# Decoder layer on one core: the residual seeds the down projection's banks, the last visits are reordered, and the weight tiles come from two pools

## The chip, the core and the metric

The kernel runs on 1 core of a Trainium2 chip. The metric is the device time of one execution in microseconds (us), as a median of runs. Five engines work side by side, each on its own list of instructions in program order: PE (TensorE, with its weight loads shown apart as PEld), DVE (VectorE), ACT (ScalarE), POOL (GpSimd) and SP (SyncE, which here issues most transfers). They wait for each other through semaphores. A transfer is issued by an engine's queue and carried by 16 DMA engines. SBUF is the memory that engines read, PSUM the banks in which TensorE accumulates.

## What is computed

One layer of a decoder, for a prompt of 512 tokens and for 8 samples of 4 tokens, with the same weights; T = 544 columns in all, in two halves of HT = 272. Attention, a gated delta rule and cross attention come first; the change lies in the feed-forward part and at the step into it:

```python
    x = x + xo @ p['w_xo']
    hf = rmsnorm(x, p['norm_ffn_g'])
    gate, up = jnp.split(hf @ p['w_gate_up'], 2, axis=-1)
    x = x + (jax.nn.silu(gate) * up) @ p['w_down']
```

The width of `x` is 2048 (KD = 16 row blocks of 128), the hidden width 5632 (NH = 44 blocks). The last `x +` is called the residual here. All of it is float32; a product of two float32 matrices is made as three products of their high and low parts, `wh*h + wh*l + wl*h`.

## The kernel before

**Into the feed-forward part.** `cross` ends with the projection `w_xo` in two parts (halves of the columns), each over m = 0 to 15: `weights` (L191) loads a tile `wr` on SP's queue (L195), ACT casts it to `wh` (L200), DVE makes `wl` (L201), TensorE multiplies (L1534), DVE adds the product to `x[m]` (L1537). Six of the sixteen weight pairs are kept from the first part to the second, in the pool `pb2`; the others come from the pool `w`. In the second part, as pairs of `x[m]` are ready, `Pair` makes the operands of the gate and up projection from them on DVE and ACT (L1586 to L1613). `x` itself is stored to `xT` in DRAM. When all of this is released, the pools `hp` and `wp` are opened over its space.

**Gate and up.** For each of the 44 hidden blocks a 2x2 block product is made in 7 products instead of 8, from sums of blocks. Each of the 7 is a tick of the plan: 24 matmuls of 128x128 by 128x272 (L1726; L1898 warms up). A weight tile goes raw (SP, L1702), `sum` (DVE, L1708), `wh` (ACT, L1715), `wl` (DVE, L1719). All of them are tiles of one size in the pool `wp`, in a ring of 13. The hidden rows go to `hT` in DRAM and come back as `pr` on POOL's queue (L1944).

**Down.** From tick 308 on, output rows are made in 8 blocks of two (m = 0, 2 ... 14), again by 7 products. A *step* is 42 matmuls (L1780) for one block and one of 11 groups of hidden rows: 88 steps. A step's weights: `raw` in two transfers (L1747), three sums on DVE (L1757 to L1759), two casts to `wh` on ACT (L1764), two `wl` on DVE (L1770). A *visit* is one or more steps of one block in a row. The products gather in four PSUM tiles, the banks P16, P7, P45 and P23. All blocks share the four, so each visit ends by taking them out to SBUF parts (`take`, L1820 adds on DVE, L1822 copies on ACT), and P45 and P23 are seeded with the next block's parts before its first product (`before`, L1802). At the last visit of a block `combine` (L1830 to L1837) joins banks and parts to the two output rows.

**Order.** `VISITS` lists (half, groups) and runs each entry over the half's four blocks. `LAST` is a last stage of end visits that alternate between block m with two steps and block m + 8 with one. There are 52 visits. Under a manual schedule, `at(tick, place, fn)` puts instructions in order by tick and then by place, on all engines alike; an engine never passes over one that waits.

**Residual.** In the two steps after the second visit of a block (the third for the other half), `residual` loads `xl` from `xT` (SP, L1846, two buffers of the tag `rstd`), POOL multiplies it by `r1` (L1851) and adds it to, or takes it off, the parts (L1853 to L1856).

**Output.** `store_y` (L2029): four transposes of a finished row to the one bank `aux` (L964), four scalings to `y` on ACT (L2036), a store (L2037); as a third piece two transposes of the sample columns (L2041), a scaling `ys` on DVE (L2043), a store (L2045). The row of P23 comes first, then that of P45.

## Time and profile before

| | before |
|---|---|
| median of 3 runs | 3003.34 us (3001.32 to 3003.95) |
| the profiled execution's own time | 3001.82 us |
| its span in the trace | 3000.1 us |
| mean granted TensorE clock | 0.988 |
| PE / PEld busy | 2881.7 us (96%) / 2772.6 us (92%) |
| DVE / ACT / POOL busy | 2096.9 us (70%) / 1490.5 us (50%) / 731.8 us (24%) |

The last matmul of `w_xo` starts at 1500.40 us of the span. Gate and up fill 1507 to 2460 us, down 2460 to 2988 us, and the last store ends the span at 3000.1 us.

How rows are read: a row of the stretches gives start and end, length, then for PE, PEld, DVE, ACT and POOL the busy us and the number of instructions, then the granted TensorE clock (1.00 is full), the busy share of the DMA engines and GB/s. (That share can read above 1.) A group row gives line, engine, operation, output <- inputs, shapes, count, busy us and mean ns of one. A row of waits gives who waited for whom, the us in total, how often and the longest.

### The profile page before, as it was taken

To read this page: it belongs to the slowest core of one execution; us is meant where nothing else is said; L and a number is where in the kernel's file an instruction comes from. 1 tells how busy PE (TensorE), PEld (TensorE's weight loads), DVE (VectorE), ACT (ScalarE), POOL (GpSimd) and SP (SyncE) were. 2 spreads that over 40 slices of the span, in tenths; PEclk is the share of its full clock that TensorE was granted. 3 is DMA by queue.
4 is the path that set the end of the run, shared out by engine and by line. 5 is a ranking of instruction groups with operands and counts; after the bars stand their busy time and mean duration, and the time that the engine had idled before them with its cause. 6 is when DMAs were issued, how large, how long until landed. Compare 5 with 4: busy or idle time off the path is not lost.

```text
span 3000.1 us, 56822 instructions
## 1 busy us (share of the span) xinstructions
PE 2881.7 (96%) x22122; PEld 2772.6 (92%) x22122; DVE 2096.9 (70%) x3302; ACT 1490.5 (50%) x2820; POOL 731.8 (24%) x932
## 2 busy tenths in 40 slices
PE   8999999999999999999979999999999999899997
PEld 7999998889899989998769999999999999899996
DVE  6776775655656664346588878888788877987765
ACT  5545443444555664345554444444444456455554
POOL 3211213312113100004213332333323333631100
PEclk9999999999999999999989999999999999999998
DMA  7323333454544674433444445454454459677542
GB/s 216 94 77 83 84 91 87 136 150 124 176 128 126 201 239 147 141 100 109 132 133 140 146 136 158 144 158 134 146 155 150 148 171 273 173 215 201 172 133 74
DMA packets 635814, 435.47 MB, mean 145 GB/s; under 512 B 35899, under 2 KB 566152, under 8 KB 635544
## 3 DMA queue, kind: packets, MB, share of 16 engines
q1 hardware_dynamic: 603720, 377.39, 43.0%
q0 software_dynamic: 22176, 42.90, 4.7%
q10 hardware_dynamic: 9648, 11.54, 1.1%
q8 instruction: 174, 2.85, 0.4%
q14 instruction: 96, 0.79, 0.1%
HBM read 355.61 MB, written 76.13 MB: 144 GB/s over the span
## 4 chain that ended last, share of the span: by engine, by line
PE 54%; DVE 5%; DMA 2%; issue 1%; ACT 1%; SPq 0%; DVEq 0%; ACTq 0%
PE gu L1726 30%; PE bank L1780 11%; PE mm L212 8%; DVE wl L1770 2%; PE aux L1346 2%; PE mm L1534 2%; DMA raw<-in_w_down 1%; PE aux L964 1%; DVE sum L1758 1%; PE aux L754 0%; DVE sum L1757 0%; DVE sum L1759 0%; DMA raw<-in_w_gate_up 0%; DVE a L1820 0%; PE aux L1420 0%
## 5 line engine op out<-in xcount | busy, mean ns | idle before, releaser
L1726 PE MATMUL gu<-pr,wh 128*128 128x272 f32 x4928 | 673.1, 289 | 13.1 <-ACT pr L1601 12.1
L1726 PEld LDWEIGHTS gu<-pr,wh 128*128 128x128 f32 x4928 | 639.6, 189 | 15.7 <-ACT pr L1601 13.3
L212 PE MATMUL mm<-ah,wh 128*128 128x272 f32 (+1 forms) x2464 | 537.8, 298 | 5.4 <-ACT ah L325 4.2
L212 PE MATMUL mm<-al,wh 128*128 128x272 f32 (+1 forms) x2464 | 523.3, 291 | 0.7 <-DVE al L243 0.6
L212 PE MATMUL mm<-ah,wl 128*128 128x272 f32 (+1 forms) x2464 | 515.0, 290 | 0.1
L1780 PE MATMUL bank<-pr,wh 128*128 128x272 f32 x2464 | 474.6, 291 | 12.6 <-ACT bank L1802 12.0
L212 PEld LDWEIGHTS mm<-ah,wh 128*128 128x128 f32 (+1 forms) x2464 | 391.1, 188 | 28.8 <-issue 8.5
L1780 PEld LDWEIGHTS bank<-pr,wh 128*128 128x128 f32 x2464 | 391.5, 191 | 14.6 <-ACT bank L1802 13.6
L201 DVE TENSOR_TENSOR wl<-wr,wh 128x512 fp32r<-128x512 f32 (+1 forms) x366 | 262.5, 721 | 194.7 <-ACT wh L200 185.4
L212 PEld LDWEIGHTS mm<-al,wh 128*128 128x128 f32 (+1 forms) x2464 | 388.7, 188 | 5.4 <-issue 2.0
L200 ACT CAST wh<-wr 128x512 fp32r<-128x512 f32 (+1 forms) x366 | 224.3, 615 | 333.2 <-PE mm L212 272.2
L212 PEld LDWEIGHTS mm<-ah,wl 128*128 128x128 f32 (+1 forms) x2464 | 385.4, 188 | 2.5 <-DVE wl L201 0.5
L1780 PE MATMUL bank<-pr,wl 128*128 128x272 f32 x1232 | 364.2, 296 | 18.7 <-DVE wl L1770 15.8
L1726 PE MATMUL gu<-pr,wl 128*128 128x272 f32 x2464 | 359.8, 288 | 1.3 <-DVE wl L1719 1.3
L1726 PEld LDWEIGHTS gu<-pr,wl 128*128 128x128 f32 x2464 | 328.9, 189 | 1.6 <-DVE wl L1719 1.6
L1719 DVE TENSOR_TENSOR wl<-sum,wh 128x1024 fp32r<-128x1024 f32 x176 | 215.9, 1226 | 83.5 <-ACT wh L1715 83.1
L1715 ACT CAST wh<-sum 128x1024 fp32r<-128x1024 f32 x176 | 185.0, 1051 | 164.2 <-DVE wl L1719 156.1
L1780 PEld LDWEIGHTS bank<-pr,wl 128*128 128x128 f32 x1232 | 235.2, 191 | 30.8 <-DVE wl L1770 30.6
L1719 DVE TENSOR_TENSOR wl<-raw,wh 128x1024 fp32r<-128x1024 f32 x132 | 201.3, 1525 | 5.2 <-ACT hs L1932 0.5
L1715 ACT CAST wh<-raw 128x1024 fp32r<-128x1024 f32 x132 | 138.9, 1053 | 95.7 <-DVE sum L1708 72.9
L1708 DVE TENSOR_TENSOR sum<-raw,sum 128x1024 f32<-128x1024 f32 x88 | 125.4, 1425 | 29.6 <-PE gu L1726 29.6
L1933 POOL TENSOR_TENSOR hs<-x,hs 128x544 fp32r<-128x544 f32 x44 | 86.3, 1962 | 184.2 <-ACT hs L1932 120.9
(524 smaller groups left out, 4397.4 us busy)
## 6 DMA issues: line engine op xcount, KB each, us to landing
raw<-in_w_gate_up SPq DMA_DIRECT2D x176, 512.0 KB
wr<-in_w_in SPq DMA_DIRECT2D x108, 512.0 KB
raw<-in_w_down SPq DMA_DIRECT2D x176, 256.0 KB
hT<-hs SPq DMA_DIRECT2D x154, 272.0 KB
pr<-hT POOLq DMA_DIRECT2D x154, 272.0 KB, 7.0
page<-in_cache_sb_k SPq DMA_DIRECT2D x128, 128.0 KB
page<-in_cache_sb_v SPq DMA_DIRECT2D x64, 256.0 KB
wr<-in_w_out SPq DMA_DIRECT2D x32, 512.0 KB
```

Of the source, the lines that this page charges most:

```text
L200: nc.scalar.copy(hi[:, :m, :n], raw[:, k : k + m, :n])
L201: nc.vector.tensor_sub(lo[:, :m, :n], raw[:, k : k + m, :n], hi[:, :m, :n].bitcast(F32))
L212: c.nc.tensor.matmul(ps[:n, h, :HT], l[:, :n], r[:, h * HT : (h + 1) * HT], start=first and i == 0, stop=last and i == 2,)
L1346: nc.tensor.matmul(ps[:, :256], l, r, start=k == 0 and n == 0, stop=k == 7 and n == 2)
L1534: nc.tensor.matmul(ps[:, 0, :HT], l, r[:, cols], start=k == 0 and i == 0, stop=k == 3 and i == 2)
L1708: self.f.c.nc.vector.tensor_sub(self.a[q], self.a[x], self.a[y])
L1715: self.f.c.nc.scalar.copy(self.hi[q], self.left(q))
L1719: self.f.c.nc.vector.tensor_sub(self.lo[q], self.left(q), self.hi[q].bitcast(F32))
L1726: self.f.c.nc.tensor.matmul(bank, w[:, i * P : (i + 1) * P], self.f.pairs[i].op[q][r], start=q in (1, 5) and n == 0, stop=n == 23, skip_gr ...
L1770: self.c.nc.vector.tensor_sub(lo, x, self.hi[i].bitcast(F32))
L1780: self.c.nc.tensor.matmul(self.c.bank[bank][:, o], t[x][:, s, i * P : (i + 1) * P], pairs[i].op[q][r], start=new and not (i or n), stop=se ...
L1933: at(tick, 80, lambda: c.nc.gpsimd.tensor_sub(lo[:, o : o + w], src[:, :w], hi[:, :w].bitcast(F32)))
```

## The change

1. The table of visits: the two-step entry of half 0 on groups 7 and 8 becomes two entries of one step, half 1 gets an entry of its own on group 8, and all end visits have two steps. 56 visits, 7 for each block.
2. `residual` is gone. `Ffn.start` runs eight times during gate and up: it loads two rows from `xT`, POOL multiplies both by `r1` and takes half of one off the other, and SP stores them to a DRAM tile `xq`. At a block's first visit, P45 and P23 are seeded from `xq` (`Down.load`, two buffers of the tag `rstd`); the order of products is then 4, 5, 1, 6, 7, 2, 3.
3. `take`: P16 and P7 always by DVE, as a copy the first time, P45 and P23 by ACT. `combine(0)` stands among the matmuls of the end visit's last step and not behind them, in two pieces; sums and the first `wl` of a step stand earlier in the tick.
4. Output: P45's row first, `ys` scaled on ACT, and the last block's transposes go to three banks that are free by then and not to `aux`.
5. Weight tiles: 9 in `wp` and 4 in a new pool `vp`, which holds every `wl` and the raw block "12". The pool `w` is opened earlier, so that other tiles of the phase before lie below the two; `weights` takes its `wh` and `wl` ahead of `wr`.

```diff
-VISITS = ((0, (0,)), (1, (0,)), (1, (1,)), (0, (1, 2)), (1, (2, 3)), (0, (3, 4)), (1, (4, 5)), (0, (5, 6)), (1, (6, 7)), (0, (7, 8)), (1, (8, 9)))
-LAST = (9, 10), (10,)
+VISITS = ((0, (0,)), (1, (0,)), (1, (1,)), (0, (1, 2)), (1, (2, 3)), (0, (3, 4)), (1, (4, 5)), (0, (5, 6)), (1, (6, 7)), (0, (7,)), (0, (8,)),
+          (1, (8,)))
+LAST = (9, 10), (9, 10)
...
 def weights(c, w, k0, nk, c0, n=P, kept=False, eng=None):
+    parts = [[(c.pb if kept else c.w).tile([P, 4, P], F32R, tag=x, name=x, bufs=XO_KEPT if kept else 4) for x in ("wh", "wl")] for _ in range(0, nk, 4)]
     raw = c.w.tile([P, 8, P], F32, tag="wr", name="wr", bufs=3)
...
-    self.a[x] = f.tile(F32, "raw")
+    self.a[x] = f.tile(F32, "raw", x == "12")
...
     def next_visit(self):
         self.visit += 1
-        self.order = (1, 6, 7, 4, 5, 2, 3) if self.visit == self.end else (4, 5, 2, 3, 1, 6, 7)
-        self.seeds = () if not self.visit else (P45, P23, P16, P7) if self.visit == self.end else (P45, P23)
+        self.order = (1, 6, 7, 4, 5, 2, 3) if self.visit == self.end else (4, 5, 2, 3, 1, 6, 7) if self.visit else (4, 5, 1, 6, 7, 2, 3)
+        self.seeds = (P45, P23, P16, P7) if self.visit == self.end else (P45, P23)
+    def load(self, bank):
+        self.x = self.x if bank == P23 else {}
+        self.x[bank] = self.c.cst.tile([P, T], F32, tag="rstd", name="xl", bufs=2)
+        self.c.nc.sync.dma_start(self.x[bank], self.f.xq[self.m + (bank == P45)])
     def before(self, bank):
         if bank in self.seeds:
-            self.c.nc.scalar.copy(self.c.bank[bank], self.parts[bank])
+            self.c.nc.scalar.copy(self.c.bank[bank], self.parts[bank] if self.visit else halves(self.x[bank]))
...
     def take(self, bank):
         new, x = bank not in self.parts, self.part(bank)
-        if bank in (P16, P7) and not new:
+        if bank in (P45, P23):
+            self.c.nc.scalar.copy(x, self.c.bank[bank])
+        elif new:
+            self.c.nc.vector.tensor_copy(x, self.c.bank[bank])
+        else:
             self.c.nc.vector.tensor_add(x, x, self.c.bank[bank])
-        else:
-            self.c.nc.scalar.copy(x, self.c.bank[bank])
...
+        for m in range(0, KD, 2):
+            for step, place in enumerate((3, 79, 2)):
+                at(38 + 14 * m + 3 * step, place, lambda m=m, step=step: self.start(m, step))
...
-        return self.c.wp.tile([P, 8 * P], dt, tag="w", name=name, bufs=W_TILES)
+        return (self.c.vp if own else self.c.wp).tile([P, 8 * P], dt, tag="w", name=name, bufs=4 if own else W_TILES - 4)
...
+    def start(self, m, step):
+        c, g = self.c, self.c.nc.gpsimd
+        if step == 0:
+            self.x = [c.tt("xr") for _ in range(2)]
+            for i, x in enumerate(self.x):
+                c.nc.sync.dma_start(x, c.xT[m + i])
+        elif step == 1:
+            for x in self.x:
+                g.tensor_mul(x, x, self.r1)
+            y, z = self.x
+            g.tensor_sub(y[:, HT:], y[:, HT:], z[:, HT:])
+        else:
+            for i, x in enumerate(self.x):
+                c.nc.sync.dma_start(self.xq[m + i], x)
...
-        at(early(2), 45, s.sums)
+        at(early(2), 25, s.sums)
         for i in range(2):
             at(early(1), 20 + i, lambda i=i: s.high(i))
-            at(early(1), 50 + i, lambda i=i: s.low(i))
+            at(early(1), (31, 50)[i], lambda i=i: s.low(i))
         if p == 0:
-            at(tick, 28, lambda: (self.c.open_banks(), b.next_visit()))
+            at(tick, 28, lambda: (self.c.open_banks(), b.next_visit(), seed(b, P45, P23)))
+            at(tick - 4, 62, lambda: b.load(P45))
+            at(tick - 1, 62, lambda: b.load(P23))
...
+        if nb and nb.m not in self.begun:
+            self.begun.add(nb.m)
+            for bank in (P45, P23):
+                at(*((tick - 1, 62) if p else (tick, 29)), lambda bank=bank: nb.load(bank))
...
         if s.visit == b.end:
-            at(tick, 47, lambda: (b.combine(0), seed(P16, P7)))
-            at(tick, 60, lambda: (b.combine(1), seed(P45)))
-            at(tick, 61, lambda: (b.combine(2), seed(P23), self.out(tick, b)))
+            at(tick, 32.2, lambda: b.combine(0))
+            at(tick, 33.2, lambda: b.combine(0.5))
+            at(tick, 34, lambda: seed(nb, P16, P7))
+            at(tick, 60, lambda: (b.combine(1), seed(nb, P45)))
+            at(tick, 61, lambda: (b.combine(2), seed(nb, P23), self.out(tick, b, nb is None)))
...
-        if s.visit == 1 + (b.m >= 8):
-            b.residual(tick)
...
-        done = [(b.m, b.flat[P23]), (b.m + 1, b.flat[P45])]
+        done = [(b.m + 1, b.flat[P45]), (b.m, b.flat[P23])]
...
+            self.work.at(t, x, lambda i=i: store_y(self.c, done, i, self.c.spare[i] if last else None))
...
+    ps = c.aux() if ps is None else ps
...
-    nc.vector.tensor_scalar(t[:NS, : 2 * P], ps[:NS, : 2 * P], c.unscale[:NS, 4:5], None, ALU.mult)
+    nc.scalar.activation(t[:NS, : 2 * P], ps[:NS, : 2 * P], AF.Identity, scale=c.unscale[:NS, 4:5])
...
     phase = ExitStack()
+    c.w = phase.enter_context(tc.tile_pool(name="w", bufs=3))
     c.pc = phase.enter_context(tc.tile_pool(name="pc", bufs=1))
...
-    c.hp, c.wp = (ctx.enter_context(tc.tile_pool(name=x, bufs=3)) for x in ("hp", "wp"))
+    c.hp, c.vp, c.wp = (ctx.enter_context(tc.tile_pool(name=x, bufs=3)) for x in ("hp", "vp", "wp"))
```

First place: SP's list where the feed-forward part begins, before the change. `wr` are the last weights of `w_xo`, `raw` the first of gate and up.

```order
L195 DMA wr<-in_w_xo 128x4x128
L1473 DMA xv<-in_cache_mem_v 128x512 x3
L195 DMA wr<-in_w_xo 128x4x128 x3
L1702 DMA raw<-in_w_gate_up 128x8x128 x15
L1935 DMA hT<-hs 128x544 x3
```

The same place of the changed kernel:

```order
L198 DMA wr<-in_w_xo 128x4x128
L1476 DMA xv<-in_cache_mem_v 128x512 x3
L1705 DMA raw<-in_w_gate_up 128x8x128 x3
L198 DMA wr<-in_w_xo 128x4x128 x3
L1705 DMA raw<-in_w_gate_up 128x8x128 x12
```

Three raw tiles of gate and up now stand ahead of the last three tiles of `w_xo`.

Second place: SP's list around the first steps of down, before the change. `raw` are the steps' weights (two rows to a step), `hT` the last hidden rows on their way out.

```order
L1935 DMA hT<-hs 128x544 x2
L1747 DMA raw<-in_w_down 128x4x128 x6
L1935 DMA hT<-hs 128x544
L1747 DMA raw<-in_w_down 128x4x128 x2
L1935 DMA hT<-hs 128x544 x2
L1747 DMA raw<-in_w_down 128x4x128 x4
L1935 DMA hT<-hs 128x544 x2
L1747 DMA raw<-in_w_down 128x4x128 x2
L1935 DMA hT<-hs 128x544 x2
L1747 DMA raw<-in_w_down 128x4x128 x16
L1846 DMA xl<-xT 128x544
L1747 DMA raw<-in_w_down 128x4x128 x2
```

The same place of the changed kernel; `xl` are the prepared residual rows:

```order
L1750 DMA raw<-in_w_down 128x4x128 x2
L1807 DMA xl<-xq 128x544 x6
L1750 DMA raw<-in_w_down 128x4x128 x2
L1807 DMA xl<-xq 128x544 x2
L1750 DMA raw<-in_w_down 128x4x128 x2
L1944 DMA hT<-hs 128x544
L1807 DMA xl<-xq 128x544 x2
L1750 DMA raw<-in_w_down 128x4x128 x2
L1944 DMA hT<-hs 128x544 x2
L1807 DMA xl<-xq 128x544 x2
L1750 DMA raw<-in_w_down 128x4x128 x2
L1807 DMA xl<-xq 128x544 x2
```

The residual's sixteen loads stood behind the first 18 steps' weights, one to a step; now they stand in pairs among the weights of the first steps.

Third place: DVE's list in the last stage, before the change. `sum` and `wl` belong to a step's weights, the `a` rows are `combine`, `ys` is the scaled piece of the samples.

```order
L1757 TENSOR_TENSOR sum<-raw 128x2x256
L1758 TENSOR_TENSOR sum<-raw,sum 128x256
L1759 TENSOR_TENSOR sum<-raw,sum 128x256
L1770 TENSOR_TENSOR wl<-raw,wh 128x768
L1770 TENSOR_TENSOR wl<-sum,wh 128x1024
L2043 TENSOR_SCALAR ys<-aux,unscale 32x256
L1757 TENSOR_TENSOR sum<-raw 128x2x256
L1758 TENSOR_TENSOR sum<-raw,sum 128x256
L1759 TENSOR_TENSOR sum<-raw,sum 128x256
L1831 TENSOR_TENSOR a_29603<-a_29605,bank_29402 128x272
L1832 TENSOR_TENSOR a_29603<-a_29603,bank_29403 128x272
L1770 TENSOR_TENSOR wl<-raw,wh 128x768
```

The same place of the changed kernel:

```order
L1760 TENSOR_TENSOR sum<-raw 128x2x256
L1761 TENSOR_TENSOR sum<-raw,sum 128x256
L1762 TENSOR_TENSOR sum<-raw,sum 128x256
L1773 TENSOR_TENSOR wl<-raw,wh 128x768
L1773 TENSOR_TENSOR wl<-sum,wh 128x1024
L1760 TENSOR_TENSOR sum<-raw 128x2x256
L1761 TENSOR_TENSOR sum<-raw,sum 128x256
L1762 TENSOR_TENSOR sum<-raw,sum 128x256
L1773 TENSOR_TENSOR wl<-raw,wh 128x768
L1842 TENSOR_TENSOR a_29786<-a_29783,bank_29486 128x272
L1844 TENSOR_TENSOR a_29786<-a_29786,bank_29487 128x272
L1773 TENSOR_TENSOR wl<-sum,wh 128x1024
```

No `ys` stands between the steps' weights, two steps' weights lie between one `combine` and the next, and the first `wl` of the next step comes ahead of `combine`.

More of the change, by code (lines that the diff above doesn't have):

```diff
@@ L198, in weights @@
         m = min(4, nk - k)
-        hi, lo = ((c.pb if kept else c.w).tile([P, 4, P], F32R, tag=x, name=x, bufs=XO_KEPT if kept else 4) for x in ("wh", "wl"))
+        hi, lo = parts.pop(0)
         nc.scalar.copy(hi[:, :m, :n], raw[:, k : k + m, :n])
@@ L958, in invert, with transposes @@
     res.append(tt)
-def transposes(c, src, n=4):
-    ps = c.aux()
+def transposes(c, src, n=4, ps=None):
+    ps = c.aux() if ps is None else ps
     for a in range(n):
@@ L1831, in combine @@
             v.tensor_add(u2, s1, c.bank[P16][:, 1])
+        elif stage == 0.5:
             v.tensor_add(u3, u2, c.bank[P7][:, 0])
@@ L2024, in ffn, with store_y @@
         f.go()
-def store_y(c, ys, step):
+def store_y(c, ys, step, ps=None):
     nc = c.nc
@@ L2187, in open_banks @@
         banks = ctx.enter_context(tc.tile_pool(name="banks", bufs=1, space=PSUM))
-        c.bank = [banks.tile([P, n, 512], F32, name=f"bank{i}")[:, :, :HT] for i, n in enumerate((2, 1, 2, 2))]
+        c.bank = [banks.tile([P, n, 512], F32, name=f"bank{i}") for i, n in enumerate((2, 1, 2, 2))]
+        c.spare = [c.bank[i][:, 0] for i in (P16, P7, P45)]
+        c.bank = [b[:, :, :HT] for b in c.bank]
     c.open_banks = open_banks
```

49 lines of the change are left out of this document (14 added, 35 removed).

## The prediction

> **What bounds the kernel now.** I read first the table of stretches, cut where the work changes, because shares over the whole span hide that the changed stages have different limits.
>
> ```profile
> 1500.70:1528.50 27.80, 7.67 (x25) 6.12 (x26) 19.46 (x32) 16.86 (x31) 7.68 (x8) 0.64 0.69 213
> 1528.50:1603.20 74.70, 71.47 (x543) 69.59 (x541) 62.28 (x74) 35.21 (x50) 12.82 (x10) 0.97 0.36 104
> 1650.00:2400.00 750.00, 750.00 (x5993) 750.00 (x5992) 602.56 (x609) 348.95 (x463) 238.26 (x143) 1.00 0.49 148
> 2460.00:2470.00 10.00, 9.61 (x76) 9.61 (x77) 9.83 (x13) 6.30 (x10) 2.94 (x3) 1.00 0.25 73
> 2470.00:2495.00 25.00, 25.00 (x202) 25.00 (x201) 17.37 (x22) 19.87 (x33) 10.51 (x15) 1.00 0.88 252
> 2495.00:2530.00 35.00, 31.14 (x228) 30.04 (x227) 20.09 (x31) 24.12 (x37) 16.71 (x32) 0.95 1.19 354
> 2530.00:2544.00 14.00, 12.49 (x98) 12.06 (x97) 12.77 (x20) 7.33 (x10) 0.00 (x0) 1.00 0.46 137
> 2544.00:2650.00 106.00, 95.78 (x708) 89.64 (x706) 104.56 (x100) 50.02 (x66) 68.45 (x62) 1.00 0.60 172
> 2660.00:2890.00 230.00, 228.80 (x1814) 227.06 (x1813) 177.62 (x262) 129.51 (x174) 37.10 (x70) 1.00 0.65 187
> 2890.00:2987.70 97.70, 83.67 (x575) 78.52 (x574) 58.05 (x95) 52.30 (x114) 0.00 (x0) 0.91 0.28 81
> 2987.70:3000.10 12.40, 3.23 (x12) 1.67 (x12) 3.43 (x7) 2.98 (x11) 0.00 (x0) 0.59 0.24 69
> ```
>
> The row from 1650 is TensorE without a gap: 750/5993 = 0.1252 us for a matmul, and a step of down is 42 x 0.1252 = 5.26 us. That is the yardstick: a stretch loses its length less 0.1252 us for each matmul in it. The start of the feed-forward part loses 24.7 and 6.7 us, gate and up nothing, the first steps of down (2460 to 2544) 0.5 + 0 + 6.5 + 1.7 = 8.7, the residual's stretch (2544 to 2650) 17.4, the long middle 2.9, the last stage (2890 to 2987.7) 25.7, and behind the last matmul come 12.4. Together 98 us; the change leaves the number of matmuls as it is, so only these can be won.
>
> **Start.** The chain of waits around 1500 us, and the rows of waits there:
>
> ```profile
> 1491.40 9.31 PE mm L1534 x60
> 1500.75 0.37 SPq L1702
> ...
> 1501.80 9.24 DMA raw<-in_w_gate_up
> 1511.07 2.36 DVE sum L1708 x2
> ```
>
> ```profile
> DVE sum L1708 <- DMA raw<-in_w_gate_up: 4.3, 2, 2.5
> ```
>
> The stretch that ends at 1481.5, with the matmuls of `w_xo` alone (PE, PEld, clock, DMA share, GB/s); the second part begins in it:
>
> ```profile
> 1470.00:1481.50 11.50, 10.65 (x72) 10.65 (x73) 0.85 0.26 97
> ```
>
> The first raw weights of gate and up are issued right behind the last `w_xo` matmul, since their tiles lie over what these read. In the changed kernel the first three lie over the kept weights, free after six of the twelve-matmul groups of the second part: the row with x72 puts that at 1481.5 us, 19 us sooner. But DVE is then what is late: it works 19.46 of the 27.8 us, so at most 8.3 us go, and 4.3 of these are the wait shown. Against it, SP's last three `w_xo` tiles now queue behind the three raw ones, and the two sums (2.36 us) stand ahead of `x` sums that the operands need. I take **-5**, near the wait shown; bounds -8 and +2.
>
> **Gate and up.** Eight times POOL gets two multiplies and one half subtraction; their rows stand in today's residual:
>
> ```profile
> L1846 SPq DMA_DIRECT2D xl<-xT x16: 338/339/504, 2541.1 to 2642.7; - x16
> L1851 POOL TENSOR_TENSOR xl<-xl,rstd x16: 1353/1362/2106, 2544.9 to 2646.0; 128x544 f32<-128x544 f32 x16
> ...
> L1854 POOL TENSOR_TENSOR a<-a,xl x8: 947/957/1477, 2549.3 to 2641.8; 128x272 f32<-128x272 f32 x8
> ```
>
> 8 x (2 x 1.36 + 0.96) = 29.4 us of POOL over some 300 us, with 32 more transfers at a DMA share of 0.49. TensorE has no gap there and DVE is idle for 147 of 750 us, which is the cover: **0**, bounds -1 and +5 (if a sixth of the 29.4 reaches TensorE).
>
> **First visits.** All sixteen `xl` loads, 272 KB each, move from 2541 to 2643 us into about 2440 to 2502. What transfers cost there and what a seed costs:
>
> ```profile
> pr<-hT POOLq DMA_DIRECT2D x56, 272.0 KB, 7.3
> ```
>
> ```profile
> L1764 ACT CAST wh<-sum 128x1024 fp32r<-128x1024 f32 x43 | 45.0, 1046 | 0.6 <-PE bank L1780 0.6
> L1764 ACT CAST wh<-raw 128x768 fp32r<-128x768 f32 x43 | 35.9, 834 | 65.3 <-PE bank L1780 56.8 <-DVE wl L1770 8.5
> L1802 ACT COPY bank<-a 128x544 f32<-128x544 f32 x44 | 27.2, 617 | 1.9
> ```
>
> There are two buffers, one for each bank, so a load waits for the seed of the block before, and a first visit is one step: issue 0.34, landing, seed 0.62 must fit into 5.26 us. The first `xl` today is issued at 2541.1 and used at 2544.9: a landing of 3.8 us fits (4.8). At the 7.3 us of `pr` in this very stretch the loop takes 8.3, 3.0 too long. Behind a waiting `xl` stand the raw weights of the fourth step on, so they have some three steps of lead left. By the stretches, the first two or three visits see a DMA share of 0.25 and the other five 0.9 to 1.2: five times 3.0 is +15. By bytes: ten loads of 279 KB in the full stretch are 2.8 MB, at 354 GB/s 7.9 us. A slower TensorE also gives the transfers time and takes part of the 8.7 us lost today. I take **+9**, nearest to the bytes; bounds -3 (all hidden, and the raw waits shrink with the new order) and +24 (eight times 3.0).
>
> **Residual's stretch.** The same DVE lines between 2544 and 2650 us, and then (second group) between 2660 and 2890:
>
> ```profile
> L1758 DVE TENSOR_TENSOR sum<-raw,sum 128x256 f32<-128x256 f32 x17 | 19.4, 1140 | 0.6
> ...
> L1820 DVE TENSOR_TENSOR a<-a,bank 128x544 f32<-128x544 f32 x8 | 5.7, 709 | 0.0
> ```
>
> ```profile
> L1770 DVE TENSOR_TENSOR wl<-sum,wh 128x1024 fp32r<-128x1024 f32 x44 | 53.6, 1218 | 0.0
> L1770 DVE TENSOR_TENSOR wl<-raw,wh 128x768 fp32r<-128x768 f32 x44 | 41.9, 951 | 0.0
> L1757 DVE TENSOR_TENSOR sum<-raw 128x512 f32<-128x512 f32 x43 | 29.6, 689 | 19.2 <-DMA raw<-in_w_down 18.6
> L1758 DVE TENSOR_TENSOR sum<-raw,sum 128x256 f32<-128x256 f32 x44 | 18.7, 425 | 1.5
> ...
> L1820 DVE TENSOR_TENSOR a<-a,bank 128x544 f32<-128x544 f32 x22 | 15.9, 721 | 29.7 <-PE bank L1780 29.7
> L1820 DVE TENSOR_TENSOR a<-a,bank 128x272 f32<-128x272 f32 x21 | 9.2, 437 | 0.4
> ```
>
> With POOL's residual beside it, DVE is 99% busy (104.56 of 106), a sum of 0.43 us takes 1.14, and TensorE waits. Without it the work is that of the middle, which loses 2.9 in 230 us, 1.3 in 106. So 17.4 falls to some 2.4, one more us kept for weights that are still behind: **-15**, bounds -17 and -10.
>
> The Trainium skill, "SBUF — State Buffer", section "Who interferes with whom", says that a DVE instruction with two SBUF inputs contends with a GpSimd instruction that reads SBUF, and one with a single SBUF input does not. The rows agree: the sum grows, the add from a bank (0.709 against 0.721) does not. The same rule speaks against the new place, whose DVE lines have two such inputs as well; that is the third rival.
>
> **Middle.** Twelve two-step visits become twelve more one-step visits in half 0 and half 1 (entries 7, 8 and 8). A step costs DVE 0.69 + 2 x 0.43 + 0.95 + 1.22 = 3.7 us, and taking two banks 0.72 + 0.44 more: 4.9 of 5.26. ACT has 1.88 of casts and four copies at about the 0.62 of L1802: 4.3. Both fit, barely; at 0.2 us late for each, **+2**, bounds -1 and +8.
>
> **Last stage.** Who waits there, and two rows of the chain:
>
> ```profile
> DVE ys L2043 <- PE aux L2041: 18.9, 6, 5.5
> ...
> ACT bank L1802 <- DVE a L1835: 18.2, 7, 2.6
> ```
>
> ```profile
> 2907.54 1.14 ACT y L2036 x4
> ...
> 2919.16 4.64 issue
> ```
>
> `ys` makes DVE wait for transposes that come late on TensorE, with the next step's sums queued behind it (the 4.64 us piece is such a stop, until `ys` goes). Two outputs have three steps: 15.8 us and some 2 us of transposes, while DVE needs 3 x 3.7 + 2 x (3 x 0.44 + 2 x 0.72) + 2 x 0.47 = 17.6 (`combine`'s adds at the price of L1820's, of the same shapes; 0.47 is the `ys` row of the next part). Any wait shows. After the change an output has two steps, 10.5 + 1.1 us, DVE 7.4 + 2.8 = 10.2, ACT 3.8 of casts + some 2.6 of seeds and a copy + 2 x 1.14 of `y` + 0.5 = 9.2. `combine(0)` comes amid the matmuls, and `ys` waits on ACT, where the next thing behind it is a cast with a step of lead. DVE at 87% still leaves some 0.8 us for each of 8 outputs: 25.7 falls to about 6.7, **-19**; bounds -24 and -12.
>
> **Behind the last matmul.**
>
> ```profile
> 2991.64 1.11 PE L964 MATMUL aux<-ident,a 128*128 128x128 f32 x4 [3.08 <-DVE ys L2043]
> ...
> 2996.39 0.61 PE L2041 MATMUL aux<-ident,a 128*32 128x128 f32 x2 [1.24 <-ACT y L2036]
> 2997.10 0.47 DVE L2043 TENSOR_SCALAR ys<-aux,unscale 32x256 f32<-32x256 f32 x1 [5.51 <-PE aux L2041]
> 2997.60 0.33 SPq L2045 DMA_DIRECT2D out<-ys  x1
> ```
>
> One `aux` bank makes a file of transposes and scalings. With three banks and P45's row first, what follows the last matmul is one add (0.8 with its semaphore), transposes 1.1, `y` 1.15, `ys` 0.5, some 0.3 of gaps, then store and landing as now, 2.5 from 2997.60 to the end: 6.4. **-6**, bounds -8 and -3.
>
> **The sum.** -5 + 0 + 9 - 15 + 2 - 19 - 6 = -34. From the profiled execution's 3001.8 (span 3000.1) that is 2967.8; the median of the runs shown is 1.5 above that execution, so **2969**.
>
> **Rivals.** (1) The residual's loads hide wholly: the early ones do at a share of 0.25, and 3.8 us of landing would fit. First visits 0 instead of +9: 2960. (2) The two-buffer loop binds at each first visit, as the 7.3 us would have it: +24 instead of +9, 2984. (3) POOL's preparation stops DVE in gate and up as it does in the residual's stretch now, and all 29.4 us reach TensorE: 2998, no difference that could be told. DVE's idle 147 us speak against it; the rule of the Trainium skill cited above, from "SBUF — State Buffer", would allow this case. (4) The last stage's waits only change engine: `ys` and `y` now stand on ACT ahead of seeds that TensorE waits for (18.2 us of such waits today). Half of the gain: 2978. (5) Slower: the ring of 4 in `vp` holds each `wl` and, for several products, the raw block "12"; then `wl` waits for TensorE's product three before, and DVE cannot run ahead. Gate and up has 308 products. The gain of 34 and 6 us more are gone from 0.13 us for each on; at 0.16 it is 2969 + 49 = 3018. Against it: a product is 24 x 0.1252 = 3.0 us, and three of them are more than a `wl` needs.
>
> **Chances.** Forecast 0.56, (1) 0.17, (2) 0.12, (4) 0.07, (3) 0.04, (5) 0.04. A difference under 0.2% (6 us) can't be told from none here. Faster is all but (3) and (5): 0.92, same 0.04, slower 0.04. For the range the bounds' distances from my values are added as squares, since the terms are independent: upward 7, 5, 15, 5, 6, 7, 3 give 20, downward 3, 1, 12, 2, 3, 5, 2 give 14: 2955 to 2989, and (1) with a good last stage reaches a little lower: 2951 to 2988.
>
> **What would show it.** Right: no POOL work beside the first 40 steps, the 0.43 us sums back at 0.43; `xl` landing at 4 to 8 us; ACT seeds waiting for `xl` in 2475 to 2502 us for some 10 us; no DVE wait for `ys`; a tail near 6.4 us. Wrong: gaps of TensorE in gate and up (rivals 3, 5), DVE waiting for a free `wl` tile, or ACT late with seeds in the last stage (4).

## The result, and the profile after

The changed kernel took 2974.53 us (median of 5 runs, 2969.34 to 2976.47); the kernel before, run beside it, 3003.34 us (5 runs, 3000.78 to 3007.53). The ratio is 0.9899, with a 95% interval of 0.9885 to 0.9914: faster by 1.0%, clear of noise. The profiled execution took 2976.47 us, its span is 2974.8 us. The forecast was 2969, its range 2951 to 2988.

To see where the time went, both traces are cut at the same points of the work and not at the same times: the first matmul of `w_xo`'s second part, its last one, the second product of gate and up, the first matmul of down, the first matmuls of the steps 16, 32 and 72, the last matmul, the end. The stretches of the kernel before (columns as in the prediction):

```profile
1470.80:1500.50 29.70, 27.48 (x192) 27.25 (x192) 23.65 (x51) 18.90 (x39) 6.04 (x6) 0.89 0.30 102
1500.50:1528.30 27.80, 7.66 (x26) 5.92 (x25) 19.46 (x32) 16.86 (x31) 7.63 (x9) 0.65 0.69 213
1528.30:2460.40 932.10, 928.26 (x7384) 926.16 (x7382) 753.33 (x773) 434.95 (x580) 289.66 (x185) 1.00 0.49 147
2460.40:2553.30 92.90, 87.54 (x672) 86.00 (x673) 68.78 (x92) 61.48 (x93) 35.68 (x52) 0.98 0.81 239
2553.30:2655.70 102.40, 91.90 (x675) 85.54 (x674) 100.82 (x97) 49.67 (x66) 66.15 (x65) 1.00 0.65 186
2655.70:2869.20 213.50, 212.30 (x1682) 210.56 (x1682) 162.82 (x241) 119.95 (x162) 37.10 (x70) 1.00 0.68 198
2869.20:2987.60 118.40, 104.39 (x741) 99.32 (x740) 74.12 (x119) 63.30 (x129) 0.00 (x0) 0.93 0.30 87
2987.60:3000.10 12.50, 3.31 (x13) 1.67 (x12) 3.43 (x7) 3.08 (x11) 0.00 (x0) 0.60 0.24 68
```

The same stretches of the changed kernel:

```profile
1474.30:1508.10 33.80, 26.68 (x192) 26.46 (x192) 27.85 (x57) 21.00 (x42) 6.20 (x6) 0.85 0.47 153
1508.10:1527.00 18.90, 7.20 (x26) 5.72 (x25) 14.83 (x26) 14.49 (x29) 9.11 (x9) 0.65 0.66 201
1527.00:2464.40 937.40, 930.03 (x7383) 927.86 (x7382) 753.62 (x774) 438.84 (x583) 286.54 (x210) 1.00 0.52 156
2464.40:2564.30 99.90, 90.34 (x672) 87.44 (x673) 73.17 (x107) 62.84 (x93) 29.74 (x49) 0.97 0.86 260
2564.30:2653.90 89.60, 86.80 (x675) 85.92 (x674) 64.98 (x97) 48.00 (x66) 14.80 (x28) 0.98 0.62 182
2653.90:2875.60 221.70, 215.66 (x1683) 213.48 (x1681) 169.61 (x255) 134.10 (x185) 36.98 (x70) 0.98 0.63 184
2875.60:2967.60 92.00, 92.00 (x743) 91.75 (x744) 71.84 (x111) 61.39 (x130) 0.00 (x0) 1.00 0.39 112
2967.60:2974.80 7.20, 1.39 (x11) 0.86 (x9) 0.72 (x1) 2.69 (x9) 0.00 (x0) 0.75 0.26 77
```

| stretch | before, us | after, us | difference |
|---|---|---|---|
| ahead of `w_xo`'s second part | 1470.8 | 1474.3 | +3.5 |
| into gate and up (two rows) | 57.5 | 52.7 | -4.8 |
| gate and up, and the turn to down | 932.1 | 937.4 | +5.3 |
| down, steps 0 to 15 | 92.9 | 99.9 | +7.0 |
| steps 16 to 31 | 102.4 | 89.6 | -12.8 |
| steps 32 to 71 | 213.5 | 221.7 | +8.2 |
| steps 72 to 87 | 118.4 | 92.0 | -26.4 |
| behind the last matmul | 12.5 | 7.2 | -5.3 |

The last stage's gain is as large as the whole: 92.0 us with TensorE busy for 92.00 of them. Three stretches got slower. One of them, steps 32 to 71, holds of the change only twelve one-step visits, the new places in the order, and the two rings of weight tiles (`wp` and `vp` with nine and four tiles, where one ring had thirteen). The first row is chance: over the two kernels and all experiments below the second part begins between 1469.9 and 1476.1 us, in no order with the edits.

In the last stage's stretch (up to the last matmul) two waits of DVE stood out before, and one of TensorE itself, for ACT's seeds (who for whom, us in total, times, longest):

```profile
DVE a L1831 <- ACT a L1830: 13.8, 4, 4.3
...
DVE ys L2043 <- PE aux L2041: 13.3, 5, 4.7
PE bank L1780 <- ACT bank L1802: 12.0, 7, 2.5
```

In the changed kernel:

```profile
DVE a L1842 <- ACT a L1841: 4.7, 5, 3.6
```

`ys` is gone from DVE, and DVE's wait for ACT's copy in `combine` fell from 13.8 to 4.7 us. ACT still waits for DVE ahead of seeds, 12.7 us in seven, but TensorE waits for seeds only once, 0.7 us.

Behind the last matmul, in the timeline:

```profile
2968.15 2.22 ACT L2047 ACTIVATE y<-bank,unscale 128x128 f32<-128x128 f32 x8 [2.95 <-PE bank L967]
...
2971.75 0.46 ACT L2055 ACTIVATE ys<-bank,unscale 32x256 f32<-32x256 f32 x1 [1.38 <-DMA out<-y]
```

All eight scalings run in one go. What ends late now is `ys`: its tile is one of the two of the tag `rstd`, and waits 1.38 us until a row `y` has been stored. Without that the tail would be near 6, an estimate (7.2 - 1.38).

In steps 16 to 31 DVE's sums are back at their price, without POOL's residual beside them:

```profile
L1761 DVE TENSOR_TENSOR sum<-raw,sum 128x256 f32<-128x256 f32 x16 | 6.8, 426 | 0.6
```

At the turn to down stands a wait that the prediction does not have. TensorE's timeline:

```profile
2458.37 3.26 PE L1729 MATMUL gu<-pr,wh 128*128 128x272 f32 x16 [2.71 <-DVE u L1677]
...
2464.39 0.52 PE L1783 MATMUL bank<-pr,wh 128*128 128x272 f32 x2 [1.25 <-ACT bank L1811]
```

The last product of gate and up waits for an addition `u` on DVE, and the first of down for ACT's seeds. Between them the granted clock is low (the row of the stretch, clock third from the right):

```profile
2458.30:2463.20 4.90, 4.77 (x24) 4.58 (x24) 1.85 (x3) 2.33 (x3) 0.00 (x0) 0.65 0.23 60
```

So the product's 24 matmuls take 4.8 us, where those of the product ahead of it take 3.2. The wait of 2.7, these 1.6 and 0.65 more of the wait for seeds (0.60 us before) are 5.0 of the turn's 5.3 us.

### The profile page after: what moved, and what is told of

It reads as the page before. It is cut to its first block, busy times and chain, and to the rows that moved or that the text cites. A ratio compares the mean times of both kernels' runs of the same rounds, so it can differ in the third digit from the quotient of the medians.

```text
span 2974.8 us, 56685 instructions
## 1 busy us (share of the span) xinstructions
PE 2872.8 (97%) x22122; PEld 2774.7 (93%) x22122; DVE 2066.3 (69%) x3318; ACT 1505.5 (51%) x2844; POOL 673.3 (23%) x916
## 4 chain that ended last, share of the span: by engine, by line
PE 76%; DVE 8%; DMA 5%; ACT 3%; issue 3%; POOL 1%; SPq 0%; ACTq 0%; DVEq 0%; POOLq 0%
PE gu L1729 31%; PE mm L215 21%; PE bank L1783 11%; DMA raw<-in_w_down 3%; PE aux L967 2%; PE aux L1349 2%; PE mm L1537 1%; PE aux L757 1%; PE aux L706 1%; DVE p L887 1%; DVE cv L1025 1%; DVE wl L1773 1%; DVE wl L204 1%; DVE g L888 1%; PE aux L527 1%
## 5 line engine op out<-in xcount | busy, mean ns | idle before, releaser
L1722 DVE TENSOR_TENSOR wl<-sum,wh 128x1024 fp32r<-128x1024 f32 x176 | 226.9, 1289 | 33.7 <-ACT wh L1718 30.0
L1722 DVE TENSOR_TENSOR wl<-raw,wh 128x1024 fp32r<-128x1024 f32 x132 | 190.1, 1440 | 0.8 <-ACT wh L1718 0.8
L1711 DVE TENSOR_TENSOR sum<-raw,sum 128x1024 f32<-128x1024 f32 x88 | 116.2, 1321 | 100.2 <-PE gu L1729 100.2
L1953 POOL DMA_DIRECT2D pr<-hT x154 | 81.8, 548 | 270.9 <-PE bank L1783 244.2
```

The costliest lines, as they stand in the source:

```text
L1711: self.f.c.nc.vector.tensor_sub(self.a[q], self.a[x], self.a[y])
L1722: self.f.c.nc.vector.tensor_sub(self.lo[q], self.left(q), self.hi[q].bitcast(F32))
L1953: self.c.nc.gpsimd.dma_start(t, self.hT[2 * g + pair, :, max(0, 2 * n - 1) + k])
```

## The experiments

Times are medians of the runs beside the kernel before. Where one run is told of, the verdict rests on stretches of its one trace. The last stage repeats well: it is 92 us in nine kernels. The other stretches differ from kernel to kernel even where no edit touches them: steps 0 to 15 took 99.9 to 102.4 us, steps 32 to 71 took 218.0 to 221.8, the way into gate and up 52.7 to 55.3, gate and up with the turn 935.1 to 937.4. Smaller differences than these can't be told from chance.

**The slow middle.** The steps can be counted off in the trace (42 matmuls each). In the changed kernel steps 22, 30, 38, 46, 54, 62 and 67 are longer than 5.26 us, by 1.7, 3.7, 3.6, 1.2, 1.1, 1.1 and 3.7. Around step 30, POOL's timeline, and the stretches:

```profile
2621.55 1.06 POOL L1953 DMA_DIRECT2D pr<-hT  x2 [33.45 <-PE bank L1783]
2623.05 3.71 POOL L1953 DMA_DIRECT2D pr<-hT  x7 [0.45 <-PE bank L1783]
```

```profile
2610.00:2620.00 10.00, 10.00 (x82) 10.00 (x81) 7.67 (x12) 5.96 (x8) 0.00 (x0) 1.00 0.37 107
2620.00:2630.00 10.00, 10.00 (x82) 10.00 (x82) 7.67 (x12) 5.94 (x8) 6.57 (x13) 1.00 0.85 250
2630.00:2640.00 10.00, 10.00 (x81) 9.82 (x79) 4.11 (x7) 4.26 (x7) 0.83 (x2) 1.00 1.03 300
2640.00:2650.00 10.00, 8.34 (x53) 8.09 (x53) 8.31 (x14) 3.56 (x4) 0.00 (x0) 0.83 0.36 105
```

The plan spreads a group's fourteen `pr` loads over seven ticks. But a place in the order is no time: POOL has waited 33 us for a tile, has nothing else in its list, and issues all of them in 10 us. The DMA share goes from 0.37 to 1.03, and DVE falls from 7.67 to 4.11 busy us. (Bursts alone are not new: in the kernel before POOL issues nine such loads in a row from 2670.37 us and ten from 2714.57, and steps 32 to 71 take 213.5 us there.)

```diff
-        self.c.nc.gpsimd.dma_start(t, self.hT[2 * g + pair, :, max(0, 2 * n - 1) + k])
+        if g > 2:
+            self.c.nc.sync.dma_start(t[:, :].bitcast(F32), self.hT[2 * g + pair, :, max(0, 2 * n - 1) + k])
+        else:
+            self.c.nc.gpsimd.dma_start(t, self.hT[2 * g + pair, :, max(0, 2 * n - 1) + k])
```

> The changed kernel, but the loads of pr for the fourth and later groups of hidden rows are issued on SP's queue among the raw weights, not on POOL's. Theory A: POOL has nothing else to do after the change, so it issues a group's fourteen loads within some 1.5 steps as soon as their tiles are free, and the raw weights of a step three steps later land late; the changed kernel's long steps 22, 30, 38, 46, 54, 62 and 67 (1.7, 3.7, 3.6, 1.2, 1.1, 1.0 and 3.8 us over 5.26) are these. On SP the loads are paced by the raw tiles: the 56 steps from step 16 to step 72 (311.3 us in the changed kernel, 315.9 before) take 295 to 300, the time falls by 12 to 16 us. Theory B: a group's bytes are too many for the time at any pace, or pr comes late itself: 307 us or more.

One run: 2953.49 us (before 3001.19). Its stretches from the first matmul of down to the last matmul:

```profile
2462.40:2557.40 95.00, 88.44 (x672) 86.03 (x673) 73.55 (x107) 62.66 (x93) 22.95 (x35) 0.98 0.89 273
2557.40:2641.60 84.20, 84.20 (x674) 84.20 (x673) 65.33 (x97) 47.73 (x66) 0.00 (x0) 1.00 0.60 181
2641.60:2852.60 211.00, 210.28 (x1683) 210.06 (x1681) 170.58 (x255) 133.62 (x186) 0.00 (x0) 1.00 0.65 199
```

Steps 16 to 71 take 295.2 us, where 56 x 5.26 are 294.6; the changed kernel has 311.3. Theory A's outcome is there: the same bytes, issued among the raw weights, which come when their tiles are free, cost nothing. The edit changes the pace and the queue at once, and no run has POOL's queue at SP's pace, so that it is the pace is argued and not shown. The time fell by 21 us and not by 12 to 16, since steps 0 to 15 gain as well (95.0 us for 99.9). SP's timeline shows the pairs:

```profile
2596.82 0.93 SPq L1750 DMA_DIRECT2D raw<-in_w_down  x2
2597.85 0.93 SPq L1954 DMA_DIRECT2D pr<-hT  x2
```

**The pools.** All of part 5 is undone.

```diff
-    c.hp, c.vp, c.wp = (ctx.enter_context(tc.tile_pool(name=x, bufs=3)) for x in ("hp", "vp", "wp"))
+    c.hp, c.wp = (ctx.enter_context(tc.tile_pool(name=x, bufs=3)) for x in ("hp", "wp"))
...
-        return (self.c.vp if own else self.c.wp).tile([P, 8 * P], dt, tag="w", name=name, bufs=4 if own else W_TILES - 4)
+        return self.c.wp.tile([P, 8 * P], dt, tag="w", name=name, bufs=W_TILES)
```

> The changed kernel with its fifth part undone: one ring of 13 weight tiles, the pool w opened where it was, wh and wl allocated behind wr. Theory A: the place of the tiles gives the gain at the start and nothing else: from the first w_xo matmul of the second part to the second product of gate and up 57.5 us as before, where the changed kernel takes 52.7; the rest as in the changed kernel, so about 5 us slower than it. That the second part began 3.5 us later in the changed kernel's trace is then chance, and comes out anywhere between 1470 and 1475 us here. Theory B: the opened pool also costs the earlier phases some 3.5 us; then the second part begins near 1471 us here and the whole is only 1 to 2 us slower. Theory C: the ring of four in vp holds gate and up or down back; then those stretches get shorter by more than 2 us.

One run: 2966.11 us, some 8 us faster than the changed kernel.

```profile
1475.20:1504.90 29.70, 27.47 (x192) 27.24 (x192) 23.86 (x51) 18.98 (x40) 6.13 (x7) 0.89 0.30 102
1504.90:1533.20 28.30, 7.80 (x27) 6.00 (x26) 19.17 (x32) 16.87 (x31) 7.06 (x8) 0.59 0.66 209
1533.20:2466.10 932.90, 928.22 (x7382) 926.10 (x7381) 779.22 (x774) 435.37 (x582) 337.79 (x210) 1.00 0.52 157
2565.60:2651.30 85.70, 84.70 (x674) 84.27 (x673) 64.92 (x97) 47.80 (x65) 14.80 (x28) 1.00 0.65 189
2651.30:2865.20 213.90, 211.43 (x1682) 210.33 (x1680) 169.68 (x255) 133.94 (x185) 37.00 (x70) 1.00 0.66 191
```

Theory A's start is there (58.0 us into gate and up), Theory B falls (the second part begins at 1475 us here), and Theory C holds: gate and up with the turn is 4.5 us shorter, and steps 16 to 71 take 299.6 us for 311.3, with the same bursts. So part 5 gives some 3 us at the start (52.7 to 55.3 us in nine kernels with two rings, 56.6 to 58.2 in five with one), gives them back at the turn (935.1 to 937.4 against 932.0 to 933.0), and makes the bursts cost more. Over all kernels with two rings and bursts, steps 16 to 71 took 306.3 to 311.3 us; over the two with one ring and bursts and without POOL's residual, 297.0 and 299.6.

Both edits together:

> The changed kernel with the pools as before and pr's loads from the fourth group on issued on SP. Theory A: the two rings cost something in down only because the loads come in bursts (steps 16 to 72 took 306 to 311 us in five kernels with two rings, 300 and 297 in two kernels with one); with paced loads steps 16 to 72 take 295 either way, and the start is the 5 us slower again: 2955 to 2960. Theory B: one ring is better in itself: at or under 2953.

2954.38 us (4 runs, 2953.16 to 2959.63), 0.9847 of before (0.9831 to 0.9863). Steps 16 to 71 take 295.1 us: with paced loads one ring and two are the same there, as Theory A has it. The start is slower as expected (56.6 us), but the turn faster (933.0), so in the whole nothing is left of part 5. Why a ring of nine suffers more from a burst was not settled. What the traces show is that, where no burst disturbs them, the raw weights of a step of odd number are issued 18.0 us ahead of their step with two rings and 19.2 with one.

**The turn.** Only the places of the first steps' sums and of step 0's first `wl` go back.

```diff
-        at(early(2), 25, s.sums)
+        at(early(2), 25 if p > 1 else 45, s.sums)
...
-            at(early(1), (31, 50)[i], lambda i=i: s.low(i))
+            at(early(1), (31, 50)[i] if p else 50, lambda i=i: s.low(i))
```

> The changed kernel, but the sums of the first two steps of down and the first wl of step 0 stand at their old places in the tick. Theory A: in the changed kernel the last product of gate and up waits 2.71 us for DVE's u behind these sums; the time from the second product of gate and up to the first matmul of down (937.4 us in the changed kernel, 932.1 before) falls to 934 or 935. Theory B: the seeds of the first two banks on ACT, which stand behind other ACT work there, take the wait over: 936.5 or more.

One run: 2972.04 us. From the second product to down:

```profile
1525.20:2460.30 935.10, 927.94 (x7383) 925.96 (x7382) 754.74 (x775) 438.69 (x583) 286.88 (x211) 1.00 0.52 156
```

935.1 for 937.4 is within Theory A's band, but `first_raw_on_pool`, with the sums at their new places, takes 935.1 as well, so the time shows no gain. The trace shows Theory B half right: TensorE doesn't wait for `u` any more, and waits for the seeds longer; the low clock moved with the wait, from the last product of gate and up into step 0, which takes 6.8 us for 5.4:

```profile
2460.28 0.82 PE L1783 MATMUL bank<-pr,wh 128*128 128x272 f32 x2 [3.40 <-ACT bank L1811]
```

```profile
2460.20:2463.00 2.80, 2.72 (x12) 2.72 (x13) 2.77 (x4) 0.57 (x2) 1.70 (x2) 0.50 0.61 182
```

So the places are not the turn's cause by themselves. The kernel before with the new places (told of below), which has one ring, takes 932.3 us here for 932.1, and `pools_as_before` 932.9. The same sums in DVE's list, in the changed kernel and then in `pools_as_before`:

```profile
2454.71 1.38 DVE L1760 TENSOR_TENSOR sum<-raw 128x512 f32<-128x512 f32 x1 [0.91 <-PE gu L1729]
```

```profile
2457.63 0.69 DVE L1759 TENSOR_TENSOR sum<-raw 128x512 f32<-128x512 f32 x1 [0.36 <-PE gu L1728]
```

The last product but one starts at 2452.51 and at 2458.44 us. With two rings the sums start 2.2 us behind it, with one ring 0.8 ahead of it: DVE, which waits for TensorE ahead of them, is held back by one product, and then the `u` behind the sums comes late. With two rings the stretch takes 935 us or more with the new places and with the old.

**The start.** The three raw tiles are taken off SP's queue, so that `w_xo`'s last tiles no longer stand behind them.

```diff
-        f.c.nc.sync.dma_start(self.a[x].rearrange("p (i m) -> p i m", m=P), w[:, :, c0 : c0 + P])
+        eng = f.c.nc.gpsimd if self.j == 0 and x != "12" else f.c.nc.sync
+        eng.dma_start(self.a[x].rearrange("p (i m) -> p i m", m=P), w[:, :, c0 : c0 + P])
```

> The changed kernel, but the first three raw weights of gate and up are issued on POOL's queue, so that the last three tiles of w_xo no longer stand behind them on SP. Theory A: TensorE's wait for these w_xo tiles (the chain has 7.67 us of DMA wr there) falls to about the 2 us of before, and the time from the first w_xo matmul of the second part to the second product of gate and up (52.7 us) falls to 46 to 49. Theory B: DVE, which has the three sums ahead of the adds of x, or the bytes themselves set the pace: 51.5 or more.

One run: 2971.03 us, and 54.8 us into gate and up, not shorter than 52.7. The queue was not the cause. SP issues the three tiles 14.1 us behind the second part's first matmul here and 12.6 in the changed kernel, both times right behind a `wl` of DVE that they wait for (5.7 and 3.2 us), and the chain shows 8.44 us of `DMA wr` for 7.67 there. So DVE sets when they are issued; why they land so late was not told apart.

**The last stage.** Four kernels for three causes: `ys` on DVE, the load of DVE (visits), the order of `wl` and `combine` on DVE (places).

```diff
-    nc.scalar.activation(t[:NS, : 2 * P], ps[:NS, : 2 * P], AF.Identity, scale=c.unscale[:NS, 4:5])
+    nc.vector.tensor_scalar(t[:NS, : 2 * P], ps[:NS, : 2 * P], c.unscale[:NS, 4:5], None, ALU.mult)
```

> The changed kernel with the samples' scaling ys back on DVE, all else new. Theory A: DVE's waits for late transposes (18.9 us in six waits before) were the main price of the last stage; from step 72 to the last matmul the time rises from 91.9 us by 8 to 16 (before: 118.4). Theory B: the price was DVE's load, three steps to two outputs; with two steps to each output ys has room, and the rise is 3 us or less.

One run: 2977.59 us.

```profile
2876.50:2968.50 92.00, 92.00 (x743) 91.77 (x744) 74.05 (x118) 59.07 (x123) 0.00 (x0) 1.00 0.39 112
```

No change at all: 92.0 us, TensorE without a gap. Then the table of visits of before, all else new:

> The changed kernel with the old table of visits (52 visits, end visits of two and one step in turn), all else new. Theory B, the load of DVE: from step 72 to the last matmul 91.9 us become 100 to 106, since DVE has 17.6 less 0.9 us of work in some 18 there and each wait shows. Theory A, ys and its waits: 95 or less.

One run: 2973.59 us.

```profile
2869.30:2962.20 92.90, 92.08 (x742) 91.32 (x740) 74.29 (x117) 65.17 (x136) 0.00 (x0) 1.00 0.37 109
```

0.9 us longer than 92.0. With the rest of the change in place the load of DVE, on which the prediction had put much of this stage, costs no more than that; only the tail is longer, 9.7 us from the last matmul to the end. Then the places:

```diff
-        at(early(2), 25, s.sums)
+        at(early(2), 45, s.sums)
...
-            at(early(1), (31, 50)[i], lambda i=i: s.low(i))
+            at(early(1), 50 + i, lambda i=i: s.low(i))
...
-            at(tick, 32.2, lambda: b.combine(0))
-            at(tick, 33.2, lambda: b.combine(0.5))
-            at(tick, 34, lambda: seed(nb, P16, P7))
+            at(tick, 47, lambda: b.combine(0))
+            at(tick, 47.1, lambda: b.combine(0.5))
+            at(tick, 47.2, lambda: seed(nb, P16, P7))
```

> The changed kernel with the old places in the tick: combine(0) behind the step's matmuls, and the sums and the first wl of a step behind it in DVE's order. A third theory for the last stage, C: a step's wl stood behind combine, which waits for a copy of ACT (18.7 us in five waits before); 91.9 us become 97 to 102. If the load or ys alone was the price: 94 or less. At the turn from gate and up to down the same places should bring the 2.3 us that late_sums_at_turn brought.

One run: 2981.13 us. Its last stage, and DVE's first wait in it:

```profile
2871.00:2971.80 100.80, 94.73 (x742) 92.04 (x742) 71.37 (x111) 61.65 (x130) 0.00 (x0) 1.00 0.35 102
```

```profile
DVE a L1842 <- ACT a L1841: 22.0, 8, 4.8
```

```profile
PE aux L967 <- ACT y L2047: 5.9, 6, 1.0
```

+8.8 us, within Theory C's 97 to 102, and DVE's wait for ACT's copy is 22.0 us for 4.7. But TensorE doesn't wait for a `wl` there, as Theory C has it: its waits are 5.9 us for ACT's `y`, ahead of transposes, and 0.7 for seeds. And 100.8 us are still 17.6 less than the 118.4 of the kernel before, with the old order of DVE. Gate and up with the turn took 935.1 us, as in `first_raw_on_pool`. Last, the kernel before with the new places alone:

```diff
-        at(early(2), 45, s.sums)
+        at(early(2), 25, s.sums)
...
-            at(early(1), 50 + i, lambda i=i: s.low(i))
+            at(early(1), (31, 50)[i], lambda i=i: s.low(i))
...
-            at(tick, 46, nb.next_visit)
+            at(tick, 29.5, nb.next_visit)
...
-            at(tick, 47, lambda: (b.combine(0), seed(P16, P7)))
+            at(tick, 32.2, lambda: b.combine(0))
+            at(tick, 34, lambda: seed(P16, P7))
```

> The kernel before with only the places in the tick changed: sums and first wl ahead of combine, combine(0) among the matmuls; old visits, ys on DVE, residual on POOL. Theory C: the order on DVE is the most of the last stage's gain, and ys and the visits each could stay: from step 72 to the last matmul 118.4 us become 93 to 102. If two of the three must go together: 108 or more.

One run: 2981.46 us, before 3001.57.

```profile
2872.60:2969.60 97.00, 93.87 (x742) 91.64 (x740) 76.39 (x123) 62.76 (x130) 0.00 (x0) 1.00 0.36 103
```

```profile
DVE ys L2044 <- PE aux L2042: 4.9, 3, 1.8
```

118.4 becomes 97.0: the order alone is enough for 21.4 of the 26.4 us, with `ys` on DVE and the old visits. Even `ys`'s own wait falls, from 13.3 to 4.9 us, and TensorE's wait for seeds from 12.0 to 0.7. So the order brings 21.4 us by itself and the rest of the change 17.6 by itself: they overlap, and either takes away most of the waits. No run tells what `ys` and the visits each bring under the old order, or what each half of the new order brings (sums and `wl` earlier, `combine` among the matmuls).

**The residual.** First the kernel before without its POOL residual; it leaves out the loads, multiplies and adds, so its output lacks that term:

```diff
-        if s.visit == 1 + (b.m >= 8):
-            b.residual(tick)
```

> The kernel before with the residual left out altogether (sixteen loads, POOL's 57 us of multiplies and adds; the output lacks that term). Theory A: POOL's work was what slowed DVE, and it also kept POOL from issuing the pr loads in one burst; so steps 16 to 32 fall from 102.4 us to 86 to 90, all DVE sums are at 0.43 us, and long steps of 6.5 to 9 us appear near steps 22 and 30. Theory B: POOL had no part in the pace of the loads: 84 to 86, no long steps there.

One run: 2985.75 us. Steps 16 to 31:

```profile
2557.40:2642.90 85.50, 84.68 (x674) 84.24 (x673) 65.05 (x97) 47.85 (x66) 14.79 (x28) 1.00 0.65 189
```

The residual cost 16.9 us where it stood (102.4 to 85.5). Theory A's second half falls: POOL issues the loads in bursts now, but with one ring only step 30 is long (6.6 us). Then the changed kernel with fourteen of the residual's sixteen loads left out; seven blocks get the first one's rows:

```diff
-        self.x = self.x if bank == P23 else {}
+        self.x = self.f.first_x = getattr(self.f, "first_x", {})
+        if bank in self.x:
+            return
```

> The changed kernel, but only the first block loads its residual rows; the other seven are seeded from the same two tiles (wrong rows, fourteen loads left out). Theory A: the loads are the price of the first visits; from the first matmul of down to step 16 the 99.9 us (99.4 to 102.4 in eight kernels of this kind but one) become 92 to 95, steps 3 to 8 are all at 5.3. Theory B: the raw weights, later on SP and in bursts, are: 98 or more.

One run: 2968.42 us; steps 0 to 15:

```profile
2465.40:2559.50 94.10, 88.31 (x673) 86.16 (x674) 73.13 (x107) 62.98 (x93) 29.69 (x49) 0.98 0.80 235
```

94.1 for 99.9: fourteen loads cost 5.8 us there, and steps 3, 4, 5, 7 and 8 are at 5.2 to 5.4 (step 6 is not). With all sixteen loads and `pr` on SP the stretch took 95.0, but steps 3, 4, 6 and 8 stayed 1.0 to 1.9 us over 5.26: what that edit wins there lies in steps 9, 11 and 12, which are 2.0 to 4.4 us over it in the kernel before too. In the changed kernel ACT waits for the `xl` loads:

```profile
ACT bank L1811 <- DMA xl<-xq: 7.1, 6, 2.8
```

**A version that beats both.** The loads on SP, and the sums of step 1 alone back at their place (`pools_as_before_sp_fetch` above, 2954.38 us, beats both as well):

```diff
-        at(early(2), 25, s.sums)
+        at(early(2), 45 if p == 1 else 25, s.sums)
```

> The changed kernel with pr's loads from the fourth group on issued on SP (as in fetch_on_sp) and the sums of step 1 alone at their old place. If both causes are as found they add: 2953.5 less some 2 us at the turn, 2950 to 2953, ratio to before 0.983. If the single look at fetch_on_sp was luck: 2958 or more.

2955.11 us (5 runs, 2951.78 to 2955.78), 0.9843 of before (0.983 to 0.9857), where the changed kernel has 0.9899 (0.9885 to 0.9914). That is above the 2950 to 2953 expected: the loads on SP hold (steps 16 to 71 in 295.1 us again), the late sum adds nothing that these runs could tell.

## Why the prediction was right, and where its steps were not

The time lies 5.5 us above the forecast, within the range. Term by term:

- **Start, -5: measured -4.8.** Without part 5 the start is 56.6 to 58.0 us again, so part 5 is the cause. The size is partly luck: the other kernels with two rings need up to 2.6 us more than this one. The step that SP's `w_xo` tiles "queue behind the three raw ones" is not shown as the cost, since taking the raw tiles off SP brought nothing.
- **Gate and up, 0: 0 inside, +5.3 with the turn.** Between 1650 and 2400 us TensorE has no gap in either trace, so the third rival's price, paid in TensorE's time, did not come. What failed is that the sum has no term for the turn, and that the rings were priced (fifth rival) for gate and up alone. There DVE is idle for 147 us between 1650 and 2400 us in both traces, but 86.0 of them are now waits of `sum` for TensorE's products, where 26.4 were before, and TensorE loses nothing by it. At the turn sums stand ahead of `u`, and it shows. With one ring and the same places the stretch is 4.5 us shorter.
- **First visits, +9: measured +7.0,** and 5.8 of it go with the loads. Taken by the bytes it was sized well; the loop's +15 was too much.
- **Residual's stretch, -15: measured -12.8.** The mechanism was right, and its size as well: without the residual the kernel before gains 16.9 there. The rest went into the long steps 22 and 30.
- **Middle, +2: measured +8.2.** (The "twelve two-step visits" are eight by the tables; the twelve one-step visits that come of them are right.) The step that failed is "Both fit, barely": it looked at DVE and ACT alone. The one-step visits cost next to nothing (211.0 us with the loads on SP); the `pr` bursts cost, with the two rings. The kernel before has the bursts too in these steps, with one ring, and takes 213.5 us; the new places, visits and bursts with one ring take 213.9. So what the sum lacks is the price of the two rings. Only in steps 16 to 31 are the bursts new: there POOL's residual had spread fourteen of these loads, and six of the next fourteen, two by two from 2577 to 2643 us.
- **Last stage, -19: measured -26.4.** "`ys` makes DVE wait" and "Two outputs have three steps" were the working. As a reason it is enough for most of the gain, and not the only one: the change without the new order brings 17.6 us, the new order without `ys` and visits 21.4, and with the order in place `ys` and the old visits can each come back at 0 to 0.9 us. The prediction has the order in half a sentence and gives it no price. The step that failed is "DVE at 87% still leaves some 0.8 us for each of 8 outputs": DVE is busy 71.84 of 92.0 us, 78%, and TensorE has no gap.
- **Behind the last matmul, -6: measured -5.3.**

The terms' errors partly cancel. In the traces the turn has +5, the middle +6, the residual's stretch +2, the first visits -2, the last stage -7, and chance ahead of all +3.5, together some 9 us; that the time lies so near is in part luck. Of the rivals none came true as told; the fifth was near, with its place wrong: a smaller ring that costs time at the turn and under bursts, and not in the 308 products.

## What to carry to other kernels

A place in an engine's order paces nothing on an engine that is otherwise idle; here loads that were to come spread cost nothing in a queue that something else holds to its pace, and little while the ring of weight tiles was one. Where an in-order engine waits, look at what stands behind the waiting instruction as well as at the load of the engine: here moving instructions ahead brought 21 us without lighter work, and the rest of the change, lighter work among it, 18 us without the move. Such gains overlap, so undo each part alone and also add each alone before giving it a price. And when a pattern or its buffers change, look at the first and the last period, where its neighbours are other instructions.

## What was not expected of the hardware

One POOL queue with fourteen loads of 272 KB in 10 us went with a DMA share of 1.03 after 0.37, and with 256 KB loads of SP's queue so late that DVE waited up to 6.1 us, 28.0 us in seven waits over steps 16 to 71; the same bytes on SP's own queue, two loads between two raw ones, gave no such wait. How much of the lateness reached TensorE depended on the ring: with one ring DVE waited 24.3 us in eight, and the steps took 299.6 us for 311.3.

A wait of TensorE of 2.0 us was followed by a low clock in some kernels and not in others: at the same place, ahead of the last product of gate and up, 2.0 us in `fetch_on_sp` was followed by a granted clock of 0.64 over that product (4.7 us), and 2.0 us in `first_raw_on_pool` and 2.3 in `visits_as_before` by full clock (3.3 and 3.2 us). The 3.40 us ahead of step 0 in `late_sums_at_turn` was followed by 0.50 over 2.8 us. And one wait can feed another: with DVE's order mended, its wait for the samples' transposes fell from 13.3 to 4.9 us though nothing had been done to these.
